# Gated linear attention by pairs of heads: gates squashed a pair ahead, projections emitted ahead of scores, merge inputs loaded in the last pair

## The chip, the cores and the metric

The program runs on one core of one Trainium2 chip. Its five engines are named as in the profile: PE (TensorE, matmuls; PEld is its weight loading), DVE (VectorE), ACT (ScalarE), POOL (GpSimd) and SP (SyncE, which issues most transfers). The metric is the time of one execution in microseconds of device time, as the median of several runs. A lower time is better.

## What is computed

The program is a two-block network. The first block and the tail (a product-key mixture of experts) are not touched. In the second block the tokens (512 of width 1024, and 256 context tokens) go through two mixers whose outputs are merged. One of them is the gated linear attention, with 8 heads of width 128:

```
q = silu(q) * DK**-0.5                    # per head, 512 tokens in column order
f = lb + (1 - lb) * sigmoid(fx)           # one fx for each direction
logf, k = log(f), 1 - f
bc = cumsum(logf) inside chunks of 64;  ref = bc at mid-chunk
scores = tril((q * exp(bc - ref)) @ (k * exp(ref - bc)).T)
o = scores @ v + (q * exp(bc)) @ S        # S: state before the chunk
S = exp(bc_last) * S + (k * exp(bc_last - bc)).T @ v      # 12 chunks, in series
o = rmsnorm(o_forward + flip(o_backward)) * silu(gate)
```

It runs forward and backward; the context's 4 chunks come first and give only the state. The outputs are merged with those of the other mixer (`oa`): `(sigmoid(g_a) * (oa @ w_pa) + sigmoid(g_b) * (ob @ w_pb)) @ w_o`. q, both fx, v, the gate and the two merge gates are all columns of one product of the tokens with `w_in`.

## The kernel before, in words

All large products are done in split form: a weight tile of 128x512 floats is loaded by SP into the ring `w_raw` (3 slots), ACT casts its high part (`w_hi`, 2 slots), DVE or POOL subtracts to get the low part (`w_lo`, 2 slots), and three matmuls per block (high by high, high by low, low by high) add up in PSUM (`acc`, 4 banks). The helper `proj2` (L1210) does this for a group of up to 512 columns of `w_in`, and calls an evacuation function for each 128 columns; `split` (L274) makes the two halves of an activation. The 8 heads go in four pairs `hg`. For a pair, `gla` (L1670) writes

- projections of 256 columns (two heads): q (L1725), fx of both directions (L1726, L1727) and v (L1749). Each takes 48 matmuls of 512 columns, and with context tokens 48 of 256 beside them. The evacuation of fx (`f_ev`, L1709) puts the Sigmoid on ACT and the scale and shift by `lb` on DVE;
- the logarithms (L1734) on ACT, with `1 - f` on POOL behind each;
- four chains, one for each head `j` and direction `d` (L1750 to L1820): a scan on DVE (`gl_lf`, L1757), exponentials on ACT, products on POOL and DVE, 8 score matmuls (`pt_s`), 6 transposes (`pt_k`) whose copies `gl_kn` are made by ACT, and then 11 state steps in series: a matmul `pt_kv` on PE and an update `gl_S` on DVE;
- after both directions of a head the output `gl_o` (L1826 to L1830), a norm of some 13 small operations on ACT and DVE up to `gl_y`, transposes `pt_o` back (L1846), and the product with the gate. The gate's projection stands behind the first head's norm (L1843).

At the end of a pair `between(hg)` (L1852) is called, which projects one group of 512 merge-gate columns (`merge_gates`, L1905) and keeps the four tiles `mgate` on chip. Then `block2_merge` (L1914) loads the eight `oa` tiles from DRAM (`oa_d`) into `oar`, splits them one by one between the weight tiles of its first product, and runs four products.

The text of the program sets no engine's order by itself: a scheduler takes the instructions that are ready and orders each engine's queue by what it reckons of their times, with the order of the text deciding priority; instructions marked with `keep_in_program_order` (the Ln, for the sake of ACT's tables) are not moved. A pool's memory can be taken by a later pool once that is closed, and the later tile's first write then waits for the last reader of what lay there.

Of the kernel before, what the change touches and what calls it, by code (L numbers as in the profile page):

```python
# [9 lines left out]
F32 = mybir.dt.float32  # L10
F32R = mybir.dt.float32r
# [3 lines left out]
AF = mybir.ActivationFunctionType  # L15
# [5 lines left out]
P = 128  # L21
D = 1024
S = 512
# [5 lines left out]
ND = 3  # L29
LAG = 36  # L30
# [150 lines left out]
class Net:  # L181
# [1488 lines left out]
    def gla(self, acts, keep, between):  # L1670


        nc, a = self.nc, self.a
# [5 lines left out]
        with ExitStack() as st:  # L1679
            pool = st.enter_context(self.pool("gla", side="right"))  # L1680
# [18 lines left out]
            for hg in range(4):  # L1699
                q, f, gate = [], [[], []], []  # L1700
# [8 lines left out]
                def f_ev(d):  # L1709
                    def g(j, ps, pc):  # L1710
                        h = hg * 2 + j
# [13 lines left out]
                self.proj2(4128 + hg * 256, 256, (main, None), q_ev)  # L1725
                self.proj2(5152 + hg * 256, 256, (main, ctx), f_ev(0))  # L1726
                self.proj2(6176 + hg * 256, 256, (main, ctx), f_ev(1))  # L1727

                lf = [[], []]
                for j in range(2):  # L1730
                    for d in range(2):
                        t = tp.tile([P, 12, 64], F32, tag=f"lf{d}{j}", name="gl_lf", bufs=1)
                        self.tc.keep_in_program_order(
                            nc.scalar.activation(out=t.rearrange("p c i -> p (c i)"), in_=f[d][j], func=AF.Ln))  # L1734
                        pts(f[d][j], f[d][j], -1.0, 1.0, op0=ALU.mult, op1=ALU.add)
                        lf[d].append(t)

                v = pool.tile([P, 6, 256], F32, tag="v", name="glv")

                def v_ev(j, ps, pc):  # L1740
                    t = tp.tile([P, 768], F32, tag="vT", name="gl_vT", bufs=1)
                    nc.scalar.copy(self.to_cols(t[:, 0:512]), self.by_rows(ps))
                    nc.vector.tensor_copy(t[:, 512:768], pc)
                    for b0, nb in ((0, 4), (4, 2)):
                        pt = self.pt("pt_v")
                        for b in range(nb):
                            nc.tensor.transpose(pt[:, b * P:(b + 1) * P], t[:, (b0 + b) * P:(b0 + b + 1) * P], self.ident)
                        nc.vector.tensor_copy(v[:, b0:b0 + nb, j * P:(j + 1) * P], pt[:, :nb * P].rearrange("p (b c) -> p b c", c=P))
                self.proj2(7200 + hg * 256, 256, (main, ctx), v_ev)  # L1749
                for j in range(2):  # L1750
                    h = hg * 2 + j
                    Sst, qd = [], []
                    for d in range(2):
# [19 lines left out]
                        xf = xh[:, 32 - early.start:][:, :S]  # L1773
                        sps = self.tr("pt_s").rearrange("p (b i) -> p b i", b=NB)
# [45 lines left out]
                        Sst.append(S8)  # L1820
                    ss = tp.tile([P, 768], F32, tag="vT", name="gl_scs", bufs=1)[:, :512].rearrange("p (b i) -> p b i", b=NB)
# [30 lines left out]
                between(hg)  # L1852
# [39 lines left out]
    def block2_mix(self):  # L1892

        a, st, hT, hcT = self.a, self.st2, self.hT2, self.hcT
        oa_d = self.dram.tile([8, P, S], F32, name="oa_d")
        self.stx.close()
        self.banks(4, 0, 4)
        with self.pool("gdp") as gp:
            self.gdn((hT, hcT), gp, oa_d)

        self.banks(4, 2, 2)
        mgates = [[], [], [], []]
        mp = st.enter_context(self.pool("mgp"))

        def merge_gates(n):  # L1905
            def ev(j, ps):
                t = mp.tile([P, S], F32, name=f"mgate{n}{j}")
                self.nc.scalar.activation(out=self.to_cols(t), in_=self.by_rows(ps), func=AF.Tanh, scale=0.5)
                mgates[n].append(t)
            self.proj(a["w_in_2"][0], 9248 + (n % 2) * 1024 + (n // 2) * 512, hT, True, ev)  # L1910
        ob = self.gla((hT, hcT), mp, merge_gates)
        return st, mgates, oa_d, ob, self.xres

    def block2_merge(self, st, mgates, oa_d, ob, xres):  # L1914
# [5 lines left out]
        mg, oa, raws = [], [], []  # L1920
        for n in range(8):
            raws.append(mr.tile([P, S], F32, tag=f"m2h{n}", name=f"oar{n}"))
            nc.sync.dma_start(out=raws[n], in_=oa_d[n])

# [7 lines left out]
        next_oa()  # L1932
        for half in range(2):
# [16 lines left out]
            self.proj(a["w_pb_2"][0], half * 512, ob, True, eb)  # L1950
        st.close()
# [478 lines left out]
```

## Time and profile before

| | |
|---|---|
| median of 3 runs | 4320.71 us (4320.67 to 4329.05) |
| the profiled execution | 4322.43 us |
| its span on the core | 4320.7 us |
| mean granted clock of PE | 0.968 of 2.4 GHz |
| stage of the gated linear attention | 2240 to 2789 us of the span |
| start of the merge | 2789 us |

The span is what the trace covers; the profiled execution is 1.7 us longer than it, and 1.7 us above the median. Times in the rows are counted from the span's start. A busy PE in such rows is one with matmuls under way, at whichever clock was granted, so a stretch is read by its busy time and its clock together.

### The profile page before, as it was taken

To read this page: it belongs to the slowest core of one execution; us is meant where nothing else is said; L and a number is where in the kernel's file an instruction comes from. 1 tells how busy PE (TensorE), PEld (TensorE's weight loads), DVE (VectorE), ACT (ScalarE), POOL (GpSimd) and SP (SyncE) were. 2 spreads that over 40 slices of the span, in tenths; PEclk is the share of its full clock that TensorE was granted. 3 is DMA by queue.
4 is the path that set the end of the run, shared out by engine and by line. 5 is a ranking of instruction groups with operands and counts; after the bars stand their busy time and mean duration, and the time that the engine had idled before them with its cause. 6 is when DMAs were issued, how large, how long until landed. Compare 5 with 4: busy or idle time off the path is not lost. (4 is left out here: it accounts for less than half of the span.)

```text
span 4320.7 us, 59079 instructions
## 1 busy us (share of the span) xinstructions
PE 4020.4 (93%) x21308; PEld 3131.5 (72%) x21309; DVE 2723.6 (63%) x6103; ACT 1691.7 (39%) x3234; POOL 1162.2 (27%) x1095
## 2 busy tenths in 40 slices
PE   8999899999998998899889899898889899999998
PEld 6576644766675456678777677676789798899886
DVE  5455455553644565787765655536988777777776
ACT  4544211544441134445543444323356233333333
POOL 2001100100021013322111212125779244444443
PEclk9999999999999998999989999999999999999999
DMA  4144698222457961212212111243245988888875
GB/s 134 30 120 143 239 419 369 83 85 76 115 190 314 420 262 49 69 47 59 58 45 57 47 52 52 66 127 117 64 161 199 333 310 291 303 295 301 288 267 195
DMA packets 342587, 739.72 MB, mean 171 GB/s; under 512 B 72512, under 2 KB 175024, under 8 KB 314640
## 3 DMA queue, kind: packets, MB, share of 16 engines
q1 hardware_dynamic: 277536, 540.54, 37.4%
q0 software_dynamic: 45376, 167.76, 10.6%
q10 hardware_dynamic: 19376, 27.57, 1.7%
q8 instruction: 171, 2.80, 0.3%
q14 instruction: 128, 1.05, 0.1%
HBM read 694.07 MB, written 41.70 MB: 170 GB/s over the span
## 5 line engine op out<-in xcount | busy, mean ns | idle before, releaser
L310 PE MATMUL acc<-rn_hi,w_lo 128*128 128x512 f32 x1224 | 505.9, 414 | 36.3 <-DVE w_lo L1227 15.2
L310 PE MATMUL acc<-rn_hi,w_hi 128*128 128x512 f32 x1224 | 507.6, 415 | 24.4 <-ACT w_hi L1226 14.5
L310 PE MATMUL acc<-rn_lo,w_hi 128*128 128x512 f32 x1224 | 500.2, 409 | 2.0 <-POOL rn_lo L277 2.0
L295 POOL TENSOR_TENSOR w_lo<-w_raw,w_hi 128x512 fp32r<-128x512 f32 x103 | 136.3, 1325 | 1043.3 <-ACT w_hi L293 842.4
L2252 ACT CAST p_hi<-p_raw 128x1024 fp32r<-128x1024 f32 x256 | 268.2, 1049 | 316.1 <-PE pu L310 217.8
L310 PE MATMUL pu<-rn_hi,p_lo 128*128 128x384 f32 x1024 | 350.2, 342 | 15.4 <-POOL p_lo L2253 11.6
L293 ACT CAST w_hi<-w_raw 128x512 fp32r<-128x512 f32 x316 | 195.7, 621 | 417.6 <-PE acc L310 308.9
L310 PE MATMUL pu<-rn_hi,p_hi 128*128 128x384 f32 x1024 | 349.1, 341 | 4.8 <-ACT p_hi L2252 4.6
L2253 DVE TENSOR_TENSOR p_lo<-p_raw,p_hi 128x1024 fp32r<-128x1024 f32 x243 | 298.1, 1227 | 81.4 <-ACT p_hi L2252 81.4
L310 PE MATMUL pu<-rn_lo,p_hi 128*128 128x384 f32 x1024 | 347.7, 340 | 0.0
L295 DVE TENSOR_TENSOR w_lo<-w_raw,w_hi 128x512 fp32r<-128x512 f32 x213 | 148.6, 698 | 264.8 <-ACT w_hi L293 259.3
L310 PE MATMUL py<-p_hi,ahi 128*128 128x512 f32 x768 | 304.4, 397 | 6.5 <-ACT ahi L276 4.7
L310 PEld LDWEIGHTS acc<-rn_hi,w_lo 128*128 128x128 f32 x1224 | 237.1, 194 | 99.9 <-DVE w_lo L1227 18.5
L310 PE MATMUL py<-p_lo,ahi 128*128 128x512 f32 x768 | 305.8, 398 | 2.1 <-DVE p_lo L2253 2.1
L310 PE MATMUL py<-p_hi,alo 128*128 128x512 f32 x768 | 305.0, 397 | 0.0
L310 PEld LDWEIGHTS acc<-rn_hi,w_hi 128*128 128x128 f32 x1224 | 237.1, 194 | 71.0 <-ACT w_hi L1226 16.6
L310 PEld LDWEIGHTS acc<-rn_lo,w_hi 128*128 128x128 f32 x1224 | 237.4, 194 | 36.0 <-POOL rn_lo L277 3.2
L2242 POOL DMA_INDIRECT eu<-in_expert_v_dram,idx x128 | 190.2, 1486 | 266.1 <-DVE py L2146 249.8
L2242 POOL DMA_INDIRECT eu<-in_expert_u_dram,idx x128 | 178.2, 1392 | 281.2 <-DVE dots L2132 267.1
L965 PE MATMUL gu<-wgu,xe 128*64 128x512 f32 x1024 | 228.5, 599 | 0.0
L310 PEld LDWEIGHTS pu<-rn_hi,p_lo 128*128 128x128 f32 x1024 | 194.7, 190 | 20.0 <-POOL p_lo L2253 13.1
L310 PEld LDWEIGHTS pu<-rn_hi,p_hi 128*128 128x128 f32 x1024 | 194.6, 190 | 11.5 <-ACT p_hi L2252 7.2
(744 smaller groups left out, 9474.3 us busy)
## 6 DMA issues: line engine op xcount, KB each, us to landing
w_raw<-in_w_in_dram SPq DMA_DIRECT2D x336, 256.0 KB
p_raw<-in_expert_u_T_dram SPq DMA_DIRECT2D x128, 512.0 KB
p_raw<-in_expert_v_dram SPq DMA_DIRECT2D x128, 512.0 KB
wgu<-in_w_exp_gate_dram SPq DMA_DIRECT2D x62, 1024.0 KB
wgu<-in_w_exp_up_dram SPq DMA_DIRECT2D x62, 1024.0 KB
wdn<-in_w_exp_down_dram SPq DMA_DIRECT2D x60, 1024.0 KB
ada_w<-in_w_ada_dram SPq DMA_DIRECT2D x96, 256.0 KB
gates_d<-gst ACTq DMA_DIRECT2D x24, 1024.0 KB
```

What stands on the lines that cost most here:

```text
L293: self.nc.scalar.copy(hi, raw)
L295: eng.tensor_tensor(lo, raw, hi.bitcast(F32), op=ALU.subtract)
L310: self.nc.tensor.matmul(ps, l, r, start=st, stop=sp or shared, skip_group_check=shared)
L965: nc.tensor.matmul(gu[64 * e:64 * e + 64, :], xe[:, c, 64 * e:64 * e + 64], wgu[e][:, :, c, :], start=c == 0, stop=c == KC - 1)
L2242: self.nc.gpsimd.indirect_dma_start(out=t, out_offset=None, in_=rows, in_offset=bass.IndirectOffsetOnAxis(ap=idx, axis=0))
L2252: self.nc.scalar.copy(hi, raw)
L2253: (eng or self.nc.vector).tensor_tensor(lo, raw, hi.bitcast(F32), op=ALU.subtract)
```

## The change

`gla` is rearranged, and the merge gates and `oa` go other ways:

1. fx is evacuated as it is (a copy on ACT for the tokens, one on DVE for the context). A new function `squash` does Sigmoid, scale and shift, Ln and `1 - f` for the four tiles of a pair, in place. It is called for the next pair behind the last chain of the present one.
2. q, fx and v of a pair are written by a generator `project`; during pair `hg` one projection of pair `hg + 1` is emitted ahead of each chain's scores (`next(nxt, None)`). Since two pairs' tiles live at once, they take turns in two pools, `gla` and `gla2`.
3. `between` is called ahead of each chain's scores, not once a pair. It projects merge gates by single groups of 128 columns (`merge_gate`, with `w_lo` on POOL): nine in pairs 0 to 2, seven in pair 3. The result goes to DRAM (`mg_d`), and the merge loads its 16 tiles back from the POOL queue.
4. In pair 3 `between` also loads `oa` tiles 0 to 6 (`NEARLY`) through the ring `w_raw` and splits them; they lie in a pool `oaq` on the left side, where `gla2` lay, which is closed at the start of pair 3.

```
+            def project(hg, q, f, vs):
+                pool = homes[hg % 2]
...
-                        nc.scalar.activation(out=self.to_cols(t[:, 0:512]), in_=self.by_rows(ps), func=AF.Sigmoid)
-                        nc.scalar.activation(out=t[:, 512:768], in_=pc, func=AF.Sigmoid)
-                        ts(t, t, ol[:, h:h + 1], lb[:, h:h + 1], op0=ALU.mult, op1=ALU.add)
+                        nc.scalar.copy(self.to_cols(t[:, 0:512]), self.by_rows(ps))
+                        nc.vector.tensor_copy(t[:, 512:768], pc)
...
+                yield self.proj2(4128 + hg * 256, 256, (main, None), q_ev)
+                yield self.proj2(5152 + hg * 256, 256, (main, ctx), f_ev(0))
+                yield self.proj2(6176 + hg * 256, 256, (main, ctx), f_ev(1))
+                yield self.proj2(7200 + hg * 256, 256, (main, ctx), v_ev)
+            def squash(hg, f):
+                for j, d in jd:
+                    h, t = hg * 2 + j, f[d][j]
+                    self.tc.keep_in_program_order(nc.scalar.activation(out=t, in_=t, func=AF.Sigmoid))
+                    ts(t, t, ol[:, h:h + 1], lb[:, h:h + 1], op0=ALU.mult, op1=ALU.add)
+                lf = [[], []]
+                for j, d in jd:
+                    t = tp.tile([P, 12, 64], F32, tag=f"lf{d}{j}", name="gl_lf", bufs=1)
+                    self.tc.keep_in_program_order(
+                        nc.scalar.activation(out=t.rearrange("p c i -> p (c i)"), in_=f[d][j], func=AF.Ln))
+                    pts(f[d][j], f[d][j], -1.0, 1.0, op0=ALU.mult, op1=ALU.add)
+                    lf[d].append(t)
+                return lf
+            made = [], [[], []], []
+            nxt = project(0, *made)
+            for _ in range(3):
+                next(nxt)
+            lf = squash(0, made[1])
+            for _ in nxt:
+                pass
+            for hg in range(4):
+                (q, f, vs), made = made, ([], [[], []], [])
+                v, gate, nxt = vs[0], [], project(hg + 1, *made) if hg < 3 else iter(())
+                if hg == 3:
+                    ast.close()
...
+                        next(nxt, None)
+                        between(hg)
                         sps = self.tr("pt_s").rearrange("p (b i) -> p b i", b=NB)
...
+                    if j == 1 and hg < 3:
+                        for _ in nxt:
+                            pass
+                        lf = squash(hg + 1, made[1])
...
+        def merge_gate(n, j):
+            def ev(_, ps, pc):
+                t = mp.tile([P, S], F32, tag="mgate", name="mgate_t", bufs=2)
                 self.nc.scalar.activation(out=self.to_cols(t), in_=self.by_rows(ps), func=AF.Tanh, scale=0.5)
+                self.nc.sync.dma_start(out=mg_d[n, j], in_=t)
+            self.proj2(9248 + (n % 2) * 1024 + (n // 2) * 512 + j * P, P, (hT, None), ev, self.nc.gpsimd)
...
+            for _ in range((turns[0] % 4 != 0) if hg < 3 else 2):
+                if todo:
+                    merge_gate(*todo.pop(0))
+            if hg == 3:
+                for n in range(len(oa), min(len(oa) + 2, NEARLY)):
+                    raw = self.ws.tile([P, 512], F32, tag="w_raw", name="w_raw", bufs=3)
+                    self.nc.sync.dma_start(out=raw, in_=oa_d[n])
+                    oa.append([pools[0].tile([P, S], F32R, name=f"oa{k}{n}") for k in "hl"])
+                    self.split(*oa[n], raw)
...
+                nc.gpsimd.dma_start(out=mgates[n][j], in_=mg_d[n, j])
...
-        next_oa()
```

The scheduler orders the rest. On PE, in the last two chains of pair 3, the rows of before had projection matmuls (`acc<-rn_...`) among the state steps up to the last eight:

```order
L1813 MATMUL pt_kv<-glv,gl_kn 128x128 x2
L310 MATMUL acc<-rn_hi,w_lo 128x512
L310 MATMUL acc<-rn_hi,w_hi 128x512
L1813 MATMUL pt_kv<-glv,gl_kn 128x128
L310 MATMUL acc<-rn_lo,w_hi 128x512
L310 MATMUL acc<-rn_hi,w_lo 128x512
L1813 MATMUL pt_kv<-glv,gl_kn 128x128 x8
L1830 MATMUL gl_o<-gl_S,gl_qd 64x128 x14
L1846 MATMUL pt_o<-ident,gl_y 128x128 x4
```

In the changed kernel the same engine has, for the same chains (both directions of the second head of pair 3, from the last of the first direction's steps on):

```order
L1841 MATMUL pt_kv<-glv,gl_kn 128x128 x5
L1827 MATMUL pt_k<-ident,gl_lf 128x128 x6
L1841 MATMUL pt_kv<-glv,gl_kn 128x128 x11
L1862 MATMUL gl_o<-gl_S,gl_qd 64x128 x14
L311 MATMUL acc_23673<-rn_hi,w_hi 128x512
L311 MATMUL acc_23673<-rn_lo,w_hi 128x512
```

Between the scores of the second direction of pair 3's first head and the last two of these rows there is none; behind that, 120 projection matmuls stand in one run, 48 for the gate of pair 3 and 72 for three merge gates.

On SP the transfers of pair 3 stand in this order in the changed kernel (`w_raw<-oa_d` is an `oa` tile, `w_raw<-in_w_in_dram` a weight tile, 2x256 for the gate and 4x128 for merge gates, `mg_d<-mgate_t` a merge gate written out):

```order
L1959 DMA w_raw<-oa_d 128x512
L1224 DMA w_raw<-in_w_in_dram 128x4x128 x2
L1941 DMA mg_d<-mgate_t 128x512
L1224 DMA w_raw<-in_w_in_dram 128x4x128 x2
L1941 DMA mg_d<-mgate_t 128x512
L1959 DMA w_raw<-oa_d 128x512
L1941 DMA mg_d<-mgate_t 128x512
L1975 DMA oar_24098<-oa_d 128x512
L1959 DMA w_raw<-oa_d 128x512
L1224 DMA w_raw<-in_w_in_dram 128x2x256 x4
L1224 DMA w_raw<-in_w_in_dram 128x4x128 x4
```

The third `oa` tile stands directly ahead of the gate's weights; the ring has three slots. On ACT the tiles from `oa` are cast here, behind the copies for the last chain:

```order
L1818 ACTIVATE gl_tot<-gl_ends 128x12
L1829 COPY gl_kn<-pt_k 64x4x128 x2
L1829 COPY gl_kn<-pt_k 64x2x128 x2
L277 CAST oah_23402<-w_raw 128x512
L277 CAST oah_23408<-w_raw 128x512
L277 CAST oah_23561<-w_raw 128x512
L1865 ACTIVATE gl_sq<-gl_o 128x512
```

ACT's rows at the end of a pair now are these, where before the Sigmoids stood with each evacuation:

```order
L1829 COPY gl_kn<-pt_k 64x2x128 x2
L1745 ACT_TABLE_LOAD
L1745 ACTIVATE glf_22542<-glf_22542 128x768
L1745 ACTIVATE glf_22912<-glf_22912 128x768
L1745 ACTIVATE glf_22545<-glf_22545 128x768
L1745 ACTIVATE glf_22915<-glf_22915 128x768
L1751 ACT_TABLE_LOAD
L1751 ACTIVATE gl_lf<-glf_22542 128x768
```

## Rows read from the trace of the kernel before

**Rows 1.** The page, part 1: busy time and share of each engine.

```profile
PE 4020.4 (93%) x21308; PEld 3131.5 (72%) x21309; DVE 2723.6 (63%) x6103; ACT 1691.7 (39%) x3234; POOL 1162.2 (27%) x1095
```

**Rows 2.** Windows: stretch, length, PE, PEld, DVE, ACT, POOL busy, PE clock, DMA share, GB/s.

```profile
2240.00:2350.00 110.00, 97.85 (x552) 78.44 (x551) 72.78 (x163) 49.90 (x93) 20.38 (x16) 0.94 0.17 48
2350.00:2495.00 145.00, 130.84 (x752) 105.75 (x752) 83.53 (x152) 58.47 (x93) 26.74 (x16) 0.98 0.18 51
2495.00:2641.00 146.00, 133.36 (x758) 108.35 (x758) 83.37 (x149) 60.17 (x95) 26.71 (x16) 0.96 0.19 52
2641.00:2740.00 99.00, 91.46 (x516) 75.21 (x515) 55.22 (x82) 41.32 (x64) 20.67 (x12) 0.95 0.18 49
2740.00:2789.00 49.00, 34.37 (x197) 26.24 (x195) 27.80 (x68) 16.57 (x29) 6.19 (x6) 0.89 0.26 81
2789.00:2900.00 111.00, 105.32 (x444) 83.87 (x444) 42.17 (x65) 29.74 (x50) 24.91 (x19) 0.99 0.32 99
```

**Rows 3.** Waits of PE, 2240 to 2789: who for whom, total us, times, longest.

```profile
PE acc L310 <- DVE w_lo L1227: 12.8, 6, 3.6
PE pt_o L1846 <- DVE gl_y L1841: 11.9, 5, 4.6
```

**Rows 4.** Timeline at pair 1's Ln: start, us, engine, line, what, [idle before].

```profile
2385.80 1.28 ACT L1734 ACT_TABLE_LOAD   x1
...
2387.10 3.04 ACT L1734 ACTIVATE gl_lf<-glf 128x768 f32<-128x768 f32 x4
...
2390.70 0.50 PE L310 MATMUL acc<-rn_hi,w_hi 128*128 128x512 f32 x1 [1.95 <-ACT w_hi L1226]
...
2395.72 0.79 PE L310 MATMUL acc<-rn_hi,w_lo 128*128 128x512 f32 x1 [3.59 <-DVE w_lo L1227]
```

**Rows 5.** Timeline, PE: the last chain of pair 3, and the merge's first product.

```profile
2767.34 0.71 PE L1813 MATMUL pt_kv<-glv,gl_kn 128*128 128x128 f32 x4 [0.20 <-ACT gl_kn L1801]
...
2773.15 0.49 PE L1813 MATMUL pt_kv<-glv,gl_kn 128*128 128x128 f32 x2 [0.44 <-DVE gl_S L1819]
...
2774.08 0.49 PE L1813 MATMUL pt_kv<-glv,gl_kn 128*128 128x128 f32 x2 [0.44 <-DVE gl_S L1819]
...
2775.39 0.79 PE L1813 MATMUL pt_kv<-glv,gl_kn 128*128 128x128 f32 x2 [0.82 <-DVE gl_S L1819]
...
2776.62 0.79 PE L1813 MATMUL pt_kv<-glv,gl_kn 128*128 128x128 f32 x2 [0.44 <-DVE gl_S L1819]
...
2777.86 3.25 PE L1830 MATMUL gl_o<-gl_S,gl_qd 128*64 128x128 f32 x28 [0.44 <-DVE gl_S L1819]
...
2792.61 0.39 PE L310 MATMUL acc<-oal,w_hi 128*128 128x512 f32 x1
...
2792.84 0.39 PE L310 MATMUL acc<-oah,w_lo 128*128 128x512 f32 x1
```

**Rows 6.** Timeline, PE: from the first head's output of pair 3 to the second's states.

```profile
2733.67 1.75 PE L1830 MATMUL gl_o<-gl_S,gl_qd 128*64 128x128 f32 x28
...
2753.47 0.39 PE L1780 MATMUL pt_s<-gl_e,gl_xh 128*128 128x64 f32 x2
2753.69 0.66 PE L1813 MATMUL pt_kv<-glv,gl_kn 128*128 128x128 f32 x4
```

**Rows 7.** Windows of 20 us at pair 1's boundary and behind pair 3's end.

```profile
2380.00:2400.00 20.00, 14.46 (x71) 12.03 (x71) 13.99 (x11) 13.32 (x20) 11.97 (x7) 0.83 0.14 39
2780.00:2800.00 20.00, 13.39 (x58) 10.42 (x55) 11.67 (x26) 7.24 (x13) 1.29 (x1) 0.79 0.31 111
```

**Rows 8.** Groups by line, 2240 to 2789: busy us, mean ns, idle before them.

```profile
L1757 DVE TENSOR_TENSOR_SCAN gl_lf<-reset,gl_lf 128x768 f32<-128x768 f32 x16 | 32.6, 2055 | 3.5 <-ACT gl_lf L1734 3.5
...
L1734 ACT ACTIVATE gl_lf<-glf 128x768 f32<-128x768 f32 x16 | 12.2, 833 | 0.0
...
L295 POOL TENSOR_TENSOR w_lo<-w_raw,w_hi 128x512 fp32r<-128x512 f32 x8 | 10.2, 1280 | 91.1 <-PE acc L310 61.6 <-ACT w_hi L293 29.6
...
L1715 DVE TENSOR_SCALAR glf<-glf,lb_o,lb_b 128x768 f32<-128x768 f32 x12 | 7.9, 679 | 24.4 <-ACT glf L1714 24.4
```

More of the change, by code (lines that the diff above doesn't have):

```diff
@@ L1710, in g @@
                     def g(j, ps, pc):
-                        h = hg * 2 + j
                         t = pool.tile([P, 768], F32, tag=f"f{d}{j}", name=f"glf{d}{j}")
-                        nc.scalar.activation(out=self.to_cols(t[:, 0:512]), in_=self.by_rows(ps), func=AF.Sigmoid)
-                        nc.scalar.activation(out=t[:, 512:768], in_=pc, func=AF.Sigmoid)
-                        ts(t, t, ol[:, h:h + 1], lb[:, h:h + 1], op0=ALU.mult, op1=ALU.add)
+                        nc.scalar.copy(self.to_cols(t[:, 0:512]), self.by_rows(ps))
+                        nc.vector.tensor_copy(t[:, 512:768], pc)
                         f[d].append(t)
                     return g
-                def g_ev(j, ps, pc):
-                    t = tp.tile([P, S], F32, tag=f"gb{j}", name="gl_gate", bufs=1)
-                    tc = self.to_cols(t)
-                    nc.scalar.activation(out=tc, in_=self.by_rows(ps), func=AF.Tanh, scale=0.5)
-                    stt(tc, tc, 1.0, self.by_rows(ps), op0=ALU.add, op1=ALU.mult)
-                    gate.append(t)
[L1725 to L1738, printed above, removed]
                 def v_ev(j, ps, pc):
+                    if j == 0:
+                        vs.append(pool.tile([P, 6, 256], F32, tag="v", name="glv"))
                     t = tp.tile([P, 768], F32, tag="vT", name="gl_vT", bufs=1)
@@ new lines, in gla, with g_ev @@
+            made = [], [[], []], []
[10 more added lines that the diff above has]
+                    ast.close()
+                def g_ev(j, ps, pc):
+                    t = tp.tile([P, S], F32, tag=f"gb{j}", name="gl_gate", bufs=1)
+                    tc = self.to_cols(t)
+                    nc.scalar.activation(out=tc, in_=self.by_rows(ps), func=AF.Tanh, scale=0.5)
+                    stt(tc, tc, 1.0, self.by_rows(ps), op0=ALU.add, op1=ALU.mult)
+                    gate.append(t)
@@ L1901, in block2_mix, with between, block2_merge @@
         self.banks(4, 2, 2)
-        mgates = [[], [], [], []]
         mp = st.enter_context(self.pool("mgp"))
-        def merge_gates(n):
-            def ev(j, ps):
-                t = mp.tile([P, S], F32, name=f"mgate{n}{j}")
+        mg_d = self.dram.tile([4, 4, P, S], F32, name="mg_d")
+        def merge_gate(n, j):
+            def ev(_, ps, pc):
+                t = mp.tile([P, S], F32, tag="mgate", name="mgate_t", bufs=2)
                 self.nc.scalar.activation(out=self.to_cols(t), in_=self.by_rows(ps), func=AF.Tanh, scale=0.5)
[L1909 to L1914, printed above, removed]
+                self.nc.sync.dma_start(out=mg_d[n, j], in_=t)
+            self.proj2(9248 + (n % 2) * 1024 + (n // 2) * 512 + j * P, P, (hT, None), ev, self.nc.gpsimd)
+        todo = [(n, j) for n in range(4) for j in range(4)]
+        turns, oa, pools = [0], [], []
+        def between(hg):
+            turns[0] += 1
+            if hg == 3 and not oa:
+                self.oa_st = ExitStack()
+                pools.append(self.oa_st.enter_context(self.pool("oaq")))
+            for _ in range((turns[0] % 4 != 0) if hg < 3 else 2):
[7 more added lines that the diff above has]
+                    self.split(*oa[n], raw)
+        ob = self.gla((hT, hcT), mp, between)
+        assert not todo
+        return st, mg_d, oa, oa_d, ob, self.xres
+    def block2_merge(self, st, mg_d, oa, oa_d, ob, xres):
         nc, a = self.nc, self.a
@@ L1919, in block2_merge @@
         op = ost.enter_context(self.pool("oap", side="right"))
-        mg, oa, raws = [], [], []
-        for n in range(8):
-            raws.append(mr.tile([P, S], F32, tag=f"m2h{n}", name=f"oar{n}"))
+        mg, raws = [], {}
+        for n in range(len(oa), 8):
+            raws[n] = mr.tile([P, S], F32, tag=f"m2h{n}", name=f"oar{n}")
             nc.sync.dma_start(out=raws[n], in_=oa_d[n])
+        mgates = [[op.tile([P, S], F32, name=f"mgate{n}{j}") for j in range(4)] for n in range(4)]
+        for n in range(4):
+            for j in range(4):
+                nc.gpsimd.dma_start(out=mgates[n][j], in_=mg_d[n, j])
         def next_oa():
```

12 lines of the change are left out of this document (6 added, 6 removed).

## The prediction

> **What bounds the kernel now.** I read the page's engine table first: TensorE (PE) is busy for 4020.4 us, 93% of the span [rows 1], so an edit pays only where PE stands idle or runs at the lower of its two clocks. Next the windows of the stage that the diff touches, cut at the last projection of each pair of heads [rows 2]. For each I add what PE idles to what the clock withholds (length times one minus the granted clock): 2240 to 2350 gives 12.2 + 6.6 = 18.8 us, pair 1's window 14.2 + 2.9 = 17.1, pair 2's 12.6 + 5.8 = 18.5, the first part of pair 3 7.5 + 5.0 = 12.5, its end (2740 to 2789) 14.6 + 5.4 = 20.0, and the start of the merge 5.7 + 1.1 = 6.8. That is **94 us lost** out of 660; the rest is matmuls which the change neither removes nor adds (their number is the same to within 0.2%). So 94 is the most that can be won, and the question is only how much of it the new order loses in turn.
>
> Third, the waits of PE in the stage [rows 3]: matmuls of a projection waiting for the low half of a weight tile on VectorE (12.8 us in 6 waits), and transposes `pt_o` waiting for the normalised `gl_y` (11.9 in 5). Behind these are two kinds of place. One is the **boundary** between pairs: ScalarE runs its table load and four Ln, VectorE goes into scans, and the weight splits of the projection stand behind both; PE waited 3.59 us there and the clock of that 20 us was 0.83 [rows 4, 7]. The other is a **chain** (scores, transposes, then 11 serial state steps for one head and direction) with no projection left to fill it: the last chain of pair 3, from 2767 on [rows 5].
>
> **The change part by part.**
>
> *Start and pair 0.* Today the start has 18.8 us of loss, and pair 0's chains share PE with little. In the new order `project(1)` gives one projection ahead of each chain's scores, and a merge gate beside it. What stays is the entry: the first Ln block (as today, 2 table loads and 8 activations), the first chain's own latency. I take a boundary's price for it, worked out below: 10 us, bounds 9 to 13. Gain about 9.
>
> *Boundaries, three of them.* The new `squash` is one block on ScalarE behind the last key copies: a table load 1.28, four Sigmoid, a load, four Ln. At 0.833 us for a 768-column activation [rows 8] (the Sigmoid isn't in the trace in this shape; the Ln row is the nearest) that is 1.28 + 3.33 + 1.28 + 3.33 = 9.2 us in which no weight tile is cast. VectorE has four scale-and-adds (0.68 us) and four scans (2.06) between the 11 state steps of that last chain. Eleven steps take 10.2 us at 0.93 [rows 5]. Inserted among them are 2.7 + 6.2 (one scan is behind the steps) and two weight splits of about 0.8, 10.5 us of VectorE; some 5 of these fit into the round trips, in which VectorE is free (PE itself idles 0.44 in each step [rows 5]). So the chain takes about 16. The order gives PE about 11 us in that time, so 5 us are idle; then `pt_o` waits about 3 for `gl_y`, and between 0 and 5 go to the clock, which fell after just such a wait [rows 4, 7]. So 8 to 13, taken at **9.5**, 28.5 for three. Today's boundary has 1.95 + 3.59 us of waits and 3.4 from the clock (0.17 of 20 us): 9. So the boundary is moved and regrouped rather than saved. If no cover at all were left, it would be the whole 16 less 2.5 of state steps, 13.5.
>
> By the rows a switch of function costs 1.28: the first Ln stands 0.02 us behind its load [rows 4]. The Trainium skill ("ScalarE: Activation LUTs", "What ACT_TABLE_LOAD costs") puts a switch at about 2.66 us, with a drain beside the load; by that each squash would be 2.8 us longer and the sum 8 us higher. The trace disagrees with it here, and the sum goes by the rows.
>
> *Inside the chains of pairs 0 to 2.* Between the boundaries today's pairs lose 17.1 - 9 = 8 and 18.5 - 9 = 9.5 us: weight splits, `pt_o` behind `gl_y` [rows 3], state steps. With 11 to 22 us of projection ahead of each score, in the order's rows for every chain, I leave 3 for each of two pairs, 6 (4 to 9). The evacuation by copy instead of Sigmoid has the same size; its work beside PE hides.
>
> *Pair 3, the bare stretch.* This is the bill. Projections of "the next pair" are empty here; what should fill three chains are the gate projection (48 matmuls) and three merge gates (72). But the order of SyncE shows three `oa` loads taking all three slots of `w_raw` ahead of those weights. A slot comes free when both halves of its `oa` tile are written; these tiles lie over pair 3's own q, f and v, and their first cast stands behind the last key copies on ScalarE, their first subtraction behind the last state step on VectorE. So no weight can be loaded until all chains are over: PE has chains alone, then 120 projection matmuls in one run. Its length, from the rows of the one bare chain that exists: 14 scores and transposes at 0.22 [rows 6], 3.1; key copies about 2, an estimate; 11 steps at 0.93 each with the high clock, 10.2, or at 1.23 with the low, 13.5 (10.5 in all from 2767.3 to 2777.9) [rows 5]; `gl_o` 1.75 at the high, 3.25 at the low [rows 5, 6]; from there to the first step of the next head 18.3 us today with fill [rows 6], most of it serial work of VectorE, so I take 14 to 16; 11 steps, 2 for key copies, 11 steps; then a subtraction, a load, a cast and a split, about 4, an estimate. With the high clock that is 58, with the low one all through 71. PE's work in it: 75 small matmuls (24 scores, 18 transposes, 33 steps) at 0.22 [rows 6], two `gl_o` at 1.75 and 16 more at 0.22, 23.5 us. Loss 34.5 to 47.5. The last bare chain began high and fell after some six of its eleven steps [rows 5]; with the ends weighed six to five that is **40**. Then 3 us for projections that begin at the low clock, as after today's end [rows 7]. With 1 for its first chain, pair 3 costs 44 against 32.5 today: 11.5 more.
>
> *The merge.* Six `oa` splits less at its start, and the first matmuls come from a busy PE, not after 20 bare us: about 3 less than today's 6.8. Against this, 16 loads of merge gates stand on the POOL queue ahead of four of the weight splits that POOL does at 1.28 us [rows 8]; the program's semaphores let eight be under way at once, and some wait for the buffers of the last chain. A late split at the third weight tile of the first projection costs 0 to 5; I take 2.5. Together 6.3.
>
> Sum: 10 + 28.5 + 6 + 44 + 6.3 = **95 us** against 94, with bounds of 79 and 121 when all ends fall together. The profiled execution took 4322.4 us, its span 4320.7, and the median of the runs is 4320.7, so one us more than that median is **4321**: I forecast no change.
>
> **The rivals.** (A) *The fill works at the boundaries too* (faster). PE has a further merge gate or v tiles cast already while ScalarE is in the squash, so that a boundary costs 4 to 5 rather than 9.5, and the start 5: 20 us less; with a bare stretch at 37, 25 less, 4296 to 4301. For it: every chain has projection ahead of its scores, and today's longest waits are on splits, not on PE's own order [rows 3]. Against: two `w_hi` buffers cover only about 11 us, and VectorE's scans sit in the state chain.
>
> (B) *The bare stretch stays at the low clock and the boundaries with it* (slower). Price 47.5 in place of 40 for the stretch, and a boundary at 12 in place of 9.5 since each drops the clock: 15 more, 4336. It decides if the clock falls in the first of the three bare chains and does not rise until the dense run: of the 20 us from 2780 the mean was 0.79 with just half a chain bare before it [rows 7]. The Trainium skill ("TensorE: Matmul & The Clock Gate", "Part 1: The HAM clock gate") says that the throttled state is the default, which activity releases; by that rule (B) is what a stretch of 60 us at 40% work does, and the fall in mid-chain agrees with it.
>
> (C) *The merge gates come back late*: the first evacuation of the merge waits for a reload. It comes after 96 matmuls at 0.23 us [rows 5], 22 us, and needs 1 MB of the 4 by then, beside weights that flow at 99 GB/s in this stretch today [rows 2]. If the 16 loads crawl at half of that, it waits 5 to 15 us: 4328 to 4335.
>
> (D) *The change does not do what it says*, in that the squash of the next pair lands on the path anyway and pair 3's loads are early but unread: that is in the sum already, as the bare stretch, and gives my forecast.
>
> **How the numbers follow.** Forecast with (D), 0.48, between 4306 and 4332; (A) 0.26; (B) 0.18; (C) 0.08. A change under 0.2% (8.6 us) can't be told from none by a measurement of this kernel. Of the forecast's chance 0.07 lies below 4312 and 0.03 above 4329. So faster 0.33, same 0.38, slower 0.29. The range leaves about a tenth on each side: 4296, inside (A), to 4342, above (B).
>
> **What would show it.** Right: in pair 3 no projection matmul between the second chain's scores and the last `gl_o`, 58 to 71 us long, its clock well under 1; three idle spots of 5 us each behind the Sigmoid block, PE else full from 2250 to the last pair; window losses of 17 to 18 us per pair falling to about 12. Wrong: projections inside pair 3's chains, or boundaries without a wait (then A); a wait of `acc` for a `w_lo` of POOL over 5 us or `mgate` waits at the merge's first evacuation (C); waits in the chains of pairs 1 and 2 as long as today's.

## The result: slower by 1.05%

The changed kernel takes 4367.82 us (median of 4 runs, 4366.23 to 4369.48) against 4320.69 us for the kernel before in the same comparison: a ratio of 1.0105, with an interval from 1.0093 to 1.0117. The forecast was 4321 with a range up to 4342, so 47 us are to be explained. The span of the profiled execution is 4365.1 us, 44.4 longer. The page's row on the engines, to be read with [rows 1]: PE is busy 20 us longer with the same number of matmuls (21309 against 21308); its mean clock is 0.963 against 0.968.

```profile
PE 4040.5 (93%) x21309; PEld 3148.6 (72%) x21309; DVE 2710.4 (62%) x6095; ACT 1702.4 (39%) x3234; POOL 1199.4 (27%) x1135
```

The windows of the stage in the changed kernel, in the columns of [rows 2]: pairs 0 to 2, each cut behind its last `gl_o`; pair 3 in two parts, cut behind its first head's `gl_o` and at the start of the merge; and the merge to the end of its fourth product:

```profile
2250.00:2403.00 153.00, 136.25 (x779) 111.90 (x779) 86.75 (x149) 63.68 (x95) 32.55 (x22) 0.98 0.21 59
2403.00:2545.00 142.00, 129.32 (x739) 105.86 (x735) 77.66 (x146) 59.84 (x91) 30.95 (x20) 0.95 0.20 54
2545.00:2688.00 143.00, 127.86 (x725) 105.14 (x726) 75.69 (x142) 60.40 (x91) 37.35 (x24) 0.94 0.20 56
2688.00:2736.00 48.00, 38.29 (x207) 29.74 (x203) 24.99 (x52) 16.47 (x28) 12.76 (x9) 0.86 0.13 39
2736.00:2826.00 90.00, 64.71 (x255) 49.23 (x256) 35.66 (x78) 25.79 (x43) 15.57 (x14) 0.70 0.21 62
2826.00:2924.00 98.00, 90.87 (x389) 73.46 (x388) 31.69 (x46) 24.08 (x39) 26.31 (x31) 0.98 0.39 131
```

Counted as in the prediction (idle of PE plus length times one minus the clock) the losses are 19.8, 19.8 and 23.7 us for pairs 0 to 2, 16.4 and 52.3 for the two parts of pair 3, 9.1 for the merge: 141, against 94 before. The difference, 47, is the whole result (47 by the medians, 44 by the two spans). Two rows say where: 2736 to 2826, with 25 us of idle and a clock of 0.70, and the three first, which should have been the gain and are not.

The waits of PE (who for whom, total us, times, longest) in pairs 0 to 2 and in pair 3, against [rows 3]. State steps waiting for `gl_S` were not among the two that headed the list before (2.8 us in four waits, from 2250 to 2640); they are now 17.5 us in ten waits. In pair 3 one wait for `gl_y` is 10.5:

```profile
PE pt_kv L1841 <- DVE gl_S L1847: 17.5, 10, 4.0
...
PE pt_o L1878 <- DVE gl_y L1873: 12.2, 2, 10.5
PE pt_kv L1841 <- DVE gl_S L1847: 9.7, 21, 0.8
```

The bare stretch itself, on PE (start, us, engine, line, what, [idle before]): the last projection matmul starts at 2716.45, the next one at 2793.59, 77 us later. Between them stand scores, transposes and state steps. The last steps are 1.23 us apart, as the slow ones in [rows 5] were:

```profile
2716.45 0.39 PE L311 MATMUL acc<-rn_hi,w_lo 128*128 128x512 f32 x1
...
2746.46 1.12 PE L1878 MATMUL pt_o<-ident,gl_y 128*128 128x128 f32 x4 [10.55 <-DVE gl_y L1873]
...
2785.73 0.79 PE L1841 MATMUL pt_kv<-glv,gl_kn 128*128 128x128 f32 x2 [0.44 <-DVE gl_S L1847]
2786.97 0.79 PE L1841 MATMUL pt_kv<-glv,gl_kn 128*128 128x128 f32 x2 [0.44 <-DVE gl_S L1847]
2788.20 2.86 PE L1862 MATMUL gl_o<-gl_S,gl_qd 128*64 128x128 f32 x28 [0.44 <-DVE gl_S L1847]
2793.59 0.51 PE L311 MATMUL acc<-rn_hi,w_hi 128*128 128x512 f32 x1 [2.53 <-ACT w_hi L1227]
```

SP's own timeline shows why nothing could fill it: from 2718.01 to 2787.85 it issues no transfer at all. The load of an `oa` tile into `w_raw` at 2713.78 took the last free slot; the next comes free with the first subtraction of an `oa` tile, which runs from 2788.06 to 2788.75, and the gate's weights stand behind the `oa` load that takes it at 2788.78:

```profile
2713.78 0.34 SPq L1959 DMA_DIRECT2D w_raw<-oa_d  x1
2718.01 0.32 SPq L1941 DMA_DIRECT2D mg_d<-mgate_t  x1
2787.85 0.32 SPq L1975 DMA_DIRECT2D oar<-oa_d  x1
2788.78 0.32 SPq L1959 DMA_DIRECT2D w_raw<-oa_d  x1
2789.38 10.45 SPq L1224 DMA_DIRECT2D w_raw<-in_w_in_dram  x6
```

The ring is not what SP itself waits for, though. The load of the eighth `oa` tile into `oar` stands ahead of these loads in SP's order, and it waits 69.4 us for the last `pt_kv`. So two things held the weights, and they let go within 1 us of each other. In the row of SP's waits from 2640 to 2830 (who for whom, total us, times, longest):

```profile
SPq L1975 <- PE pt_kv L1841: 69.4, 1, 69.4
```

### The profile page after: what moved, and what is told of

Read it like the earlier page. It is cut to its first block, busy times and chain, and to the rows that moved or that the text cites. A ratio compares the mean times of both kernels' runs of the same rounds, so it can differ in the third digit from the quotient of the medians.

```text
span 4365.1 us, 59147 instructions
## 1 busy us (share of the span) xinstructions
PE 4040.5 (93%) x21309; PEld 3148.6 (72%) x21309; DVE 2710.4 (62%) x6095; ACT 1702.4 (39%) x3234; POOL 1199.4 (27%) x1135
## 3 DMA queue, kind: packets, MB, share of 16 engines
q14 instruction: 128, 1.05, 0.1%
## 5 line engine op out<-in xcount | busy, mean ns | idle before, releaser
L296 POOL TENSOR_TENSOR w_lo<-w_raw,w_hi 128x512 fp32r<-128x512 f32 x95 | 125.5, 1323 | 925.1 <-ACT w_hi L294 782.7
L294 ACT CAST w_hi<-w_raw 128x512 fp32r<-128x512 f32 x284 | 175.7, 621 | 378.4 <-PE acc L311 268.7
L311 PEld LDWEIGHTS acc<-rn_hi,w_lo 128*128 128x128 f32 x1224 | 238.2, 195 | 93.0 <-POOL w_lo L1228 17.9
L296 DVE TENSOR_TENSOR w_lo<-w_raw,w_hi 128x512 fp32r<-128x512 f32 x189 | 133.9, 709 | 267.6 <-ACT w_hi L294 256.8
L1227 ACT CAST w_hi<-w_raw 128x512 fp32r<-128x512 f32 (+1 forms) x177 | 109.5, 622 | 272.6 <-PE acc_c L311 104.7
```

The source lines that it names most:

```text
L294: self.nc.scalar.copy(hi, raw)
L296: eng.tensor_tensor(lo, raw, hi.bitcast(F32), op=ALU.subtract)
L311: self.nc.tensor.matmul(ps, l, r, start=st, stop=sp or shared, skip_group_check=shared)
L1227: nc.scalar.copy(hi, raw)
```

## The experiments

All medians are device microseconds; the kernel before took 4327.4, 4330.2 and 4325.6 us (25, 15 and 25 runs) in the three comparisons that follow, so ratios to it are what can be compared. Where a kernel's stage is meant, the sums are again those of windows.

### Does a full ring stop pair 3?

**own_ring** takes the `oa` tiles out of the weight ring:

```
-NEARLY = 7
+NEARLY = 6
-                    raw = self.ws.tile([P, 512], F32, tag="w_raw", name="w_raw", bufs=3)
+                    raw = mp.tile([P, 512], F32, tag="oa_raw", name="oa_raw", bufs=2)
```

> The changed kernel, with the early oa tiles in a ring of their own (two buffers beside the merge gates' pool) instead of w_raw; six tiles instead of seven, since a seventh does not fit. Theory 1: in the changed kernel PE had no projection from 2718.7 to 2793 us because three oa tiles held all of w_raw. Then the gate's weights load at once here, projections stand among the state steps of pair 3 again, the 51.5 us at the low clock shrink to about 10, and the time falls by 25 to 38 us from 4367.8, to 4330 to 4343. Rival 1: pair 3 is bare because it has too little projection left for four chains, whatever ring is used; then the time falls by less than 10, 4358 or more.

Measured: 4330.16 us, 1.0006 of before (0.9995 to 1.0018). It falls by 38 us, or by 43 if the two ratios are compared: the upper end of theory 1's 25 to 38 or somewhat beyond it, and rival 1 is out. The six early tiles still lie over pair 3's own q, f and v. Weights now flow through pair 3, and the loads into `oar` stand behind them on SP:

```profile
2726.79 25.57 SPq L1224 DMA_DIRECT2D w_raw<-in_w_in_dram  x6
...
2792.05 0.80 SPq L1975 DMA_DIRECT2D oar<-oa_d  x2
```

**nearly2** and **nearly3** leave the ring shared and change one number, so that two or three tiles are loaded early:

```
-NEARLY = 7
+NEARLY = 2      # nearly2
+NEARLY = 3      # nearly3
```

> The changed kernel with two oa tiles loaded early instead of seven, still through w_raw; the other six are loaded and split in the merge as before. Theory 1: one slot of the ring stays free, so the weights of pair 3 flow, one at a time; 4332 to 4346. If the early tiles cost by their number (loads, casts and subtractions in pair 3), five sevenths of the loss in pair 3 would go, some 22 us, 4346. Rival 1: no change beyond 10 us, 4358 or more.

> The changed kernel with three oa tiles loaded early: just as many as w_raw has slots. Theory 1 (a full ring stops the weights): one tile more than nearly2 brings the whole bare stretch back, 35 to 45 us above nearly2, some 1.0% above the kernel before. If early tiles cost by their number, it is 3 to 8 us above nearly2.

Measured: nearly2 4324.84 us, 0.9998 of before (0.9981 to 1.0015), 7 us below the range that theory 1 gave it; nearly3 4366.76 us, 1.0087 (1.0066 to 1.0108), inside its range. One tile more costs 42 us (38 by the ratios), and three is the number of the ring's slots. It is no matter of how many tiles are loaded: from three to seven nothing clear of the noise is added (4366.8 and 4367.8; the intervals of the ratios overlap). SP in pair 3, in nearly2 (one row) and then in nearly3:

```profile
2714.53 32.19 SPq L1224 DMA_DIRECT2D w_raw<-in_w_in_dram  x7
```

```profile
2707.30 10.21 SPq L1224 DMA_DIRECT2D w_raw<-in_w_in_dram  x2
2717.81 0.34 SPq L1941 DMA_DIRECT2D mg_d<-mgate_t  x1
2722.23 0.34 SPq L1959 DMA_DIRECT2D w_raw<-oa_d  x1
...
2795.38 0.80 SPq L1975 DMA_DIRECT2D oar<-oa_d  x2
2796.31 1.57 SPq L1224 DMA_DIRECT2D w_raw<-in_w_in_dram  x3
```

In nearly2 the rows `w_raw<-in_w_in_dram` go on (seven of them in 32 us); in nearly3 there is none from 2717 until 2796, and a third `oa` load at 2722.23 is the last thing that enters the ring.

The order of SP changed along with the ring. In own_ring and nearly2 the loads into `oar` stand behind the weights of pair 3 (at 2792.05 and 2781.50); in the changed kernel and in nearly3 they stand ahead of them and wait for the last `pt_kv` (69.4 and 68.5 us). No run moves them alone. The full ring is enough to explain the stretch, since it let go after `oar` did in the changed kernel; whether `oar` ahead of the weights would have made the same stretch with a slot free was not tested.

**nearly0** loads none early, and splits the first in front of the merge as the kernel before did:

```
-NEARLY = 7
+NEARLY = 0
...
+        next_oa()
         for half in range(2):
```

> The changed kernel with no oa tile loaded early; all eight go as in the kernel before, the first split ahead of the merge's first product. Theory 1: pair 3 as in nearly2, but the last transposes have no merge matmuls to hide behind, so 5 to 8 us more than nearly2: 4338 to 4352. If the early tiles are harmful in any number, it is faster than nearly2.

Measured: 4334.35 us, 1.0019 of before (1.0006 to 1.0033), 9.5 us above nearly2, where theory 1 had 5 to 8. The last `pt_o` waits 4.6 us for `gl_y` here and not at all in nearly2. So the early loads do what the change wanted: with two tiles at hand the merge's first matmuls stand ahead of the last `pt_o` and cover its wait. Two are enough for that.

### Why do pairs 0 to 2 gain nothing?

nearly2 has pair 3 mended and still equals the kernel before. By windows it loses 62 us in pairs 0 to 2 (54 before) and 30 in pair 3 and the merge (39 before), so the projections ahead and the squash together gave nothing in pairs 0 to 2. Three kernels built on nearly2 ask why, and a fourth undoes a part. **sq_early** writes the squash ahead of the last chain:

```
...
                         k, bc = f[d][j], lf[d][j]
+                        if j == 1 and d == 1 and hg < 3:
+                            lf2 = squash(hg + 1, made[1])
...
-                        lf = squash(hg + 1, made[1])
+                        lf = lf2
```

> As nearly2, and the squash of the next pair is written ahead of the last chain's scan instead of behind that chain (one more buffer for the last logarithm tile). Theory 2: in the changed kernel a boundary loses 12 to 15 us since four scans of 2 us stand among the state steps of a chain with no projection beside it; ahead of the last chain the projection of v stands beside them, so each of three boundaries loses 4 to 5 less: 12 to 15 us below nearly2. Rival 2: VectorE's work is only moved, and the wait turns up in the last chain's scores; within 4 us of nearly2.

**tanh_late** leaves it where it was and takes the Sigmoid out of it (sigmoid as a Tanh, as q and the gate have it already); **tanh_early** has both edits:

```
...
-                        nc.scalar.copy(self.to_cols(t[:, 0:512]), self.by_rows(ps))
-                        nc.vector.tensor_copy(t[:, 512:768], pc)
+                        h = hg * 2 + j
+                        nc.scalar.activation(out=self.to_cols(t[:, 0:512]), in_=self.by_rows(ps), func=AF.Tanh, scale=0.5)
+                        nc.scalar.activation(out=t[:, 512:768], in_=pc, func=AF.Tanh, scale=0.5)
+                        ts(t, t, ol[:, h:h + 1], lb[:, h:h + 1], op0=ALU.mult, op1=ALU.add)
...
```

> As nearly2, but the gates are squashed at their evacuation by a Tanh (half the sum of one and the Tanh of half the argument, with the constants halved), so that behind the last chain only four Ln, the scans and one table load less are left. Theory 2 (the scans of VectorE among the state steps set the boundary): within 5 us of nearly2. Rival 3 (the block of Sigmoid, table load and scale-and-add sets it, 4.6 us of ScalarE and 2.7 of VectorE a boundary): 9 to 20 us faster than nearly2.

> Both together: sq_early with the Tanh at the evacuation. Theory 2: the block is hidden behind the projection of v already, so within 4 us of sq_early. Rival 3: 5 to 12 us faster than sq_early.

Measured: sq_early 4303.76 us, 0.9946 of before (0.9925 to 0.9967); tanh_late 4308.80, 0.9958 (0.9941 to 0.9976); tanh_early 4303.53, 0.9942 (0.9920 to 0.9964). sq_early gained 21 us on nearly2, more than theory 2 gave it. But tanh_late, in which theory 2 expected nothing and rival 3 expected 9 to 20, gained 16: the scans of VectorE still stand among the state steps there, and theory 2 falls as it was put. (Rival 3 in turn had tanh_early 5 to 12 us below sq_early, and it equals it: once the block is out of the last chain, shortening it gains nothing more.) What both edits have in common is ScalarE, and the four scale-and-adds of VectorE that go with the Sigmoid; these are over by 2528.4 in nearly2, before PE runs out of projections at 2529. ScalarE's rows behind the last chain's key copies (`gl_kn`) in nearly2, and then in tanh_late:

```profile
2520.78 1.93 ACT L1829 COPY gl_kn<-pt_k 64x512 f32<-64x512 f32 x4 [2.74 <-PE pt_k L1827]
2522.72 1.28 ACT L1745 ACT_TABLE_LOAD   x1
2524.02 3.05 ACT L1745 ACTIVATE glf<-glf 128x768 f32<-128x768 f32 x4
2527.09 1.28 ACT L1751 ACT_TABLE_LOAD   x1
2528.38 3.04 ACT L1751 ACTIVATE gl_lf<-glf 128x768 f32<-128x768 f32 x4
2531.33 1.12 ACT L1227 CAST w_hi<-w_raw 128x512 fp32r<-128x512 f32 x2
```

```profile
2522.85 1.93 ACT L1829 COPY gl_kn<-pt_k 64x512 f32<-64x512 f32 x4 [2.75 <-PE pt_k L1827]
2524.80 1.28 ACT L1751 ACT_TABLE_LOAD   x1
2526.10 3.05 ACT L1751 ACTIVATE gl_lf<-glf 128x768 f32<-128x768 f32 x4
2529.05 0.60 ACT L1227 CAST w_hi<-w_raw 128x512 fp32r<-128x512 f32 x1
```

In nearly2 no weight tile is cast from 2520.78 to 2531.33, in tanh_late from 2522.85 to 2529.05; 4.3 us less, which is the Sigmoid and one table load. PE has two cast tiles in hand, which is 24 matmuls of 512 columns, the first at 2518.90 in nearly2; these run out there at 2529 (the next starts at 2532.28) and not in tanh_late. The windows from first state step to `gl_o` show it (nearly2, then tanh_late):

```profile
2522.76:2540.26 17.50, 12.16 (x55) 8.84 (x53) 13.96 (x22) 11.15 (x14) 7.60 (x4) 0.80 0.09 19
```

```profile
2524.84:2541.30 16.46, 14.35 (x69) 10.04 (x67) 12.89 (x18) 8.15 (x10) 9.39 (x5) 1.00 0.18 44
```

PE idles 5.3 us with a clock of 0.80 in one, 2.1 with the full clock in the other, while VectorE is as busy in both (80 and 78% of the window). When weights flow, a scan of some 2 us between two state steps hides behind projection matmuls; it showed as a wait for `gl_S` because nothing else was left. The scans still have a part in that: in nearly2 both tiles are cast by 2532.45, but the first low half is made behind two scans (the second is in the rows), and PE gets its next `w_lo` product at 2537.51:

```profile
2534.22 2.07 DVE L1782 TENSOR_TENSOR_SCAN gl_lf<-reset,gl_lf 128x768 f32<-128x768 f32 x1
...
2536.45 1.00 DVE L1228 TENSOR_TENSOR w_lo<-w_raw,w_hi 128x512 fp32r<-128x512 f32 x1
```

So ScalarE's block decides when the casts come, and VectorE's queue adds some 4 us behind them; no run takes the scans away alone.

**before_tanh** makes the same replacement in the kernel before:

```
...
-                        nc.scalar.activation(out=self.to_cols(t[:, 0:512]), in_=self.by_rows(ps), func=AF.Sigmoid)
-                        nc.scalar.activation(out=t[:, 512:768], in_=pc, func=AF.Sigmoid)
+                        nc.scalar.activation(out=self.to_cols(t[:, 0:512]), in_=self.by_rows(ps), func=AF.Tanh, scale=0.5)
+                        nc.scalar.activation(out=t[:, 512:768], in_=pc, func=AF.Tanh, scale=0.5)
```

> The kernel before with one edit: the gates are squashed at their evacuation with a Tanh in place of the Sigmoid (constants halved), which saves a table load a pair. If the gain of tanh_late and tanh_early (16 to 25 us below before) came from the Tanh itself, this is 8 us or more faster than before. Theory 6 (it came from what a pair's order can hide, and the Sigmoids cost nothing at the evacuation): within 4 us of before.

Measured: 4329.01 us, 0.9999 of before (0.9986 to 1.0011). The Tanh alone is worth nothing; a Sigmoid at the evacuation was hidden. It cost only where the change had put it.

**no_next** drops the projections ahead of the scores:

```
-                        next(nxt, None)
```

> As nearly2, but the projections of the next pair are not written ahead of each chain's scores; they all stand behind the last chain, ahead of the squash, as far as the scheduler leaves them there. Theory 4 (writing them ahead is what fills the chains): chains have merge gates alone beside them, 8 to 15 us more in each of three pairs, 24 to 45 us slower than nearly2. Rival 4 (the scheduler fills the chains anyway, since in the kernel before the projections stood among state steps without it): within 6 us of nearly2.

Measured: 4340.36 us, 1.0028 of before (1.0016 to 1.0040), 15 us above nearly2 (13 by the ratios). Neither theory has it: the scheduler does fill part of the chains by itself, and writing the projections ahead is worth the rest, about 5 us a pair. The squash behind the last chain cost as much or more (16 and 21 us in tanh_late and sq_early), so the two cancelled.

### Parts alone, and what would be faster

**before_gates** takes the merge gates alone into the kernel before: one group of 128 columns ahead of each chain's scores, tiles kept on chip.

```
+                        between(hg)
                         sps = self.tr("pt_s").rearrange("p (b i) -> p b i", b=NB)
...
-                between(hg)
...
+            self.proj2(9248 + (n % 2) * 1024 + (n // 2) * 512 + j * P, P, (hT, None), ev, self.nc.gpsimd)
```

> The kernel before with the merge gates alone taken from the change: single groups of 128 columns, one ahead of each chain's scores, low halves on GpSimd; the results stay on chip. Theory 7 (fill beside each chain, but the gates' squash and projections stay at the pair's end): 0 to 8 us faster than before. Rival 7 (merge gates ahead of every score take the fill away from the last chain of pair 3, which has eight bare steps now and eleven then): 4 to 12 us slower.

Measured: 4315.89 us, 0.9980 of before (0.9970 to 0.9990). About 9 us faster: theory 7, at the end of its 0 to 8 or just beyond. That it comes from fill beside the chains is theory 7's reading; its windows are not taken apart here.

**more3** and **both** move merge gates from pairs 0 to 2 into pair 3, in sq_early and in tanh_early:

```
-            for _ in range((turns[0] % 4 != 0) if hg < 3 else 2):
+            for _ in range((turns[0] % 4 in (2, 3)) if hg < 3 else 3):
```

> As sq_early, with two merge gates in each of pairs 0 to 2 and ten in pair 3 instead of three and seven. Theory 5 (pair 3 loses its 15 to 20 us because its last chains have too little projection): 5 to 10 us faster than sq_early. Rival 5 (the last chain's 11 state steps are bare by the order whatever is left, and the pairs before lose their fill): same or up to 6 us slower.

> tanh_early with the merge gates spread as in more3: what would beat both kernels. If the remaining loss is that of the last chain of pair 3 and of the waits for the normalised output, which neither edit moves, it is within 4 us of tanh_early, some 0.6% below the kernel before.

Measured: more3 4304.49 us, 0.9941 of before (0.9917 to 0.9964), the same as sq_early; both 4313.23, 0.9968 (0.9955 to 0.9981), 10 us above tanh_early by the medians. Theory 5 falls: with three merge gates more, pair 3 of more3 loses 24 us by windows, against 19 in sq_early, and pairs 1 and 2, with one less each, lose 9 and 10 against 14 each. What is left in pair 3 is not a lack of matmuls. That both lies 10 us above tanh_early, where within 4 was expected, is open: its pair 3 loses 28 us against 20, but its stage as a whole only 4 more.

sq_early, tanh_early and more3 beat the kernel before by 0.5 to 0.6% of the time, and the changed kernel by about 1.6%. The windows of sq_early's pairs 1 and 2, and of its pair 3, in the columns of [rows 2]:

```profile
2411.00:2547.00 136.00, 126.23 (x744) 103.94 (x742) 76.56 (x146) 59.75 (x90) 31.59 (x21) 0.97 0.22 57
2547.00:2683.00 136.00, 125.98 (x738) 103.87 (x734) 73.42 (x142) 60.95 (x91) 34.89 (x25) 0.97 0.22 59
2683.00:2727.00 44.00, 40.34 (x234) 31.86 (x231) 27.00 (x56) 17.83 (x32) 14.12 (x10) 0.96 0.24 67
2727.00:2777.00 50.00, 40.24 (x218) 30.13 (x214) 28.12 (x56) 20.45 (x33) 14.38 (x13) 0.92 0.25 74
```

By the same count these are losses of 13.9 and 14.1 us for a pair (19.8 and 23.7 in the changed kernel), and 19 for the whole of pair 3 (68.7).

## Why the prediction was wrong

**Right: the place and its cause.** The step on pair 3 named the three `oa` loads, the order of SP, the release behind the last state step, and 120 projection matmuls in one run behind it. own_ring, nearly2 and nearly3 show that cause: taking it away is worth 38 to 43 us. What the step did not name is the load into `oar` ahead of the weights, which holds SP almost as long as the ring does.

**Wrong: the size of that stretch.** It was taken at 40 us of loss with bounds of 34.5 to 47.5, pair 3 at 44 in all. Windows give 68.7: 6 ahead of the stretch, 60 in it and 3 behind it, as forecast. So the whole stage lost 141 us, where even the upper bound of the sum was 121. Three pieces make the difference of 25 (some 14 from the length, 6.5 from PE's work, 5 from the part ahead), the first with a part of its own:

- The length was bounded by 58 to 71, and 77 us were measured. The steps all ran at the low clock from 2727 on (0.50 from 2740 to 2790 in the row below), so the upper bound was the nearer one, and the 40 had stood for about 63.5. The weighing of high and low steps, six to five, was taken from a chain that had projections until just before it; of the three chains of this stretch only the first has such a beginning (steps 0.93 apart from 2722.89 to 2725.68). In its mechanism that is rival (B), which had 0.18; but its price, 4336, is 32 us short of what was measured.

```profile
2740.00:2790.00 50.00, 32.79 (x122) 24.81 (x124) 19.00 (x48) 8.91 (x17) 4.12 (x3) 0.50 0.02 6
```

- Part of that length is the way from the first head's `gl_o` to the second head's first step: 19.6 us (2735.92 to 2755.52), where 14 to 16 were taken because no fill would stand in it. The wait for `gl_y` alone is 10.5, since the small operations of the norm wait on VectorE behind the next head's wide ones. From `gl_ms` to the start of `gl_y` they take 8.9 us here, and 4.6 in the norm at the end of pair 3 (2791.74 to 2796.36). In these rows (start, us) the norm's `gl_ms`, `gl_rs` and `rq_t` stand among such operations as `gl_lf`:

```profile
2736.82 0.69 DVE L1867 TENSOR_REDUCE gl_ms<-gl_sq 128x4 f32<-128x512 f32 x1 [3.61 <-ACT gl_sq L1865]
2737.42 0.95 DVE L1820 TENSOR_TENSOR gl_lf<-gl_ends,gl_lf 128x768 f32<-128x768 f32 x1
2738.28 1.23 DVE L1869 TENSOR_SCALAR gl_ms<-gl_ms 128x4 f32<-128x4 f32 x1
...
2743.18 1.22 DVE L273 SCALAR_TENSOR_TENSOR gl_rs<-rq_t,gl_rs 128x4 f32<-128x4 f32 x1
2744.44 0.16 DVE L271 TENSOR_TENSOR rq_t<-gl_rs 128x4 f32<-128x4 f32 x1
...
2745.72 0.69 DVE L1873 TENSOR_TENSOR gl_y<-gl_o,gl_rs 128x512 f32<-128x512 f32 x1
```

- PE's own work in the stretch was priced at 23.5 us. By the count of windows it is worth 17 at the full clock (77.1 us, 47.9 busy, a clock of 0.60), which makes 6.5 us more of the same length a loss.
- The part of pair 3 ahead of the stretch was given 1 us. From 2688 to 2716 it lost 6 (28 us with 23.8 busy and a clock of 0.94), nearly all of it the end of the last boundary.

**Wrong: pairs 0 to 2.** The start, three boundaries and the chains were to lose 44.5 us; they lost 63.3. The step that failed is the boundary, the 28.5 in that sum. In windows of 40 us round the three boundaries, in the columns of [rows 2], the loss is 13.5, 17.7 and 17.9, where 8 to 13 was the bound:

```profile
2390.00:2430.00 40.00, 30.12 (x162) 23.20 (x160) 33.16 (x52) 19.03 (x30) 17.69 (x10) 0.91 0.18 47
2530.00:2570.00 40.00, 30.66 (x152) 24.00 (x150) 31.62 (x49) 18.86 (x30) 17.61 (x10) 0.79 0.14 40
2670.00:2710.00 40.00, 28.87 (x141) 21.88 (x140) 29.93 (x47) 20.53 (x30) 21.72 (x13) 0.83 0.13 40
```

That is 49 in all (5.6 of the last lies in pair 3's window): 30 of it is idle, against some 24 in the sum, and 19 the clock, against 4.5. What PE lacked there was work. The step reads "So the chain takes about 16. The order gives PE about 11 us in that time". In the changed kernel the last chain of pair 2 takes 18.9 us from its first step (2666.62) to `gl_o` (2685.50), and 22 projection matmuls stand in it, 5 us at 0.23, not 11. The 11 us were wrong by the order itself: four weight tiles serve the gate's 48 matmuls, so a tile serves 12, and two `w_hi` slots hold 24, some 5.5 us. I had written that no tile is cast for 9.2 us and still gave PE twice what two tiles hold. In the trace just 24 matmuls run from 2662.78 to 2673.16, and the next starts at 2681.26. The other terms were near: by windows the start (2250 to 2280) and pair 0's chains lose 9.6 and 3.4 against 10 with bounds of 9 to 13, and the chains of pairs 1 and 2 lose 3.2 and 3.7 against 3 each.

**The other rivals.** (A) asked for weights cast while ScalarE is in the squash; sq_early had to move the block to get that. (C) did not happen as a late reload: the merge lost 9.1 against the forecast 6.3, half of it in one wait of PE, 4.8 us, for a `w_lo` of POOL behind the reloads, which was in the sum at 2.5. (D), by which the squash lands on the path and pair 3's loads bring nothing, is what happened; its cost is what was too small. On the table loads the rows were right: in nearly2's rows above the first Sigmoid starts at 2524.02, 0.02 us behind a load that began at 2522.72 and took 1.28, with no drain beside it. The Trainium skill ("ScalarE: Activation LUTs", "What ACT_TABLE_LOAD costs") puts a switch at 2.66 us, drain included, and the trace does not agree. The Trainium skill's "TensorE: Matmul & The Clock Gate" ("Part 1: The HAM clock gate"), by which the clock is low unless activity releases it, agrees with the row for 2740 to 2790 above: 50 us at 0.50, which is 1.2 GHz.

## What to carry to other kernels

A prefetch that shares a small ring with the stream that keeps the main engine fed cost nothing here with two of three slots, and stopped the stream with the third, since its release hung on something late: count slots against early loads before anything else, and look at what else stands ahead of the stream on the same queue. When a block of work is moved on an engine that also prepares the main engine's operands, its price depends on how long the operands in hand last, so count them in the main engine's instructions; move it beside the longest run of such work or cut it. A term that leans on the clock should be priced from a stretch as idle as the one expected, and taken at that end.

## What the runs showed of the hardware that I had not expected

An operation of VectorE on 128x4 elements takes 0.16 us in the norm (`rq_t` at 2744.44 above), but 1.23 us (2738.28) and 1.22 us (2743.18) where GpSimd multiplies tiles of 128x512 at the same time, from 2736.24 to 2739.49 and from 2742.80 to 2744.38. Both end 0.02 us behind the GpSimd operation that they overlap, and the same two lines take 0.17 and 0.16 us in the norm at the end of pair 3 (2792.46 and 2793.47), with GpSimd idle. Other operations of VectorE in the same time were not longer (`gl_ms` at 2736.82 takes 0.69 us in both norms). That the two are slow because of GpSimd is read from the overlap alone; no run tested it.

```profile
2736.24 3.25 POOL L1813 TENSOR_TENSOR gl_qd<-glq,gl_qd 128x512 f32<-128x512 f32 x2 [15.30 <-ACT gl_qd L1812]
2742.80 1.58 POOL L1791 TENSOR_TENSOR gl_e<-glq,gl_e 128x512 f32<-128x512 f32 x1 [3.31 <-ACT gl_e L1787]
```
